# Squared-relu feed-forward: pairs of feature blocks by seven quadrant products

## The chip, the cores and the metric

One core of a Trainium2 chip runs the whole program. The metric is the time of one execution in microseconds (us), as the median of several runs. The core's engines each have an instruction queue that is worked off in order: PE (TensorE, matmuls), PEld (its weight loads), ACT (ScalarE), DVE (VectorE), POOL (GpSimd) and SP (which issues the DMAs). An instruction that waits for another engine holds up everything behind it in its own queue.

## What is computed

A network of two blocks on 512 tokens of width 1024, in fp32. The second block has two layers, and each ends in the feed-forward that the change concerns:

```
h = rms_norm_2(x, ffn_norm_g[layer])
x = x + jnp.square(jax.nn.relu(h @ w_ff1[layer])) @ w_ff2[layer]
```

`w_ff1` is 1024 x 4096 and `w_ff2` 4096 x 1024. The 4096 features are taken as 32 blocks of 128.

## The kernel before

**Products.** Each fp32 operand is kept as a high part (its cast to fp32r) and a low part (the rest), and each product is three matmuls, high by high, high by low, low by high (`mm3`, lines 163 to 165). A weight is loaded as fp32 into one of 3 buffers `raw` (`load`, DMA on SP), then `cut` makes the high part by a cast on ACT (line 150) and the low part by a subtraction on DVE (line 151), both 128x1024, in one of 5 buffers `ws`. `split_to` does the same for activations (cast at line 169, subtraction at line 170).

**The feed-forward** (`ffn2`, one call a layer, stages 6 and 9 of the program). The normalised tokens lie transposed in `hT`, as [128, 2 parts, 8 blocks of the width, 512 tokens]. The up-product of one feature block (`up`) is 8 x 3 matmuls of a 128x128 weight by 512 tokens. Its relu runs on ACT (line 1487, out of a PSUM bank), the square on DVE (line 1488), the split on ACT and DVE. `ff_head` has done tokens 256 to 511 of blocks 0 to 2 ahead; `ffn2` first does their tokens 0 to 255 ("the heads", 3 x 24 matmuls of 256 columns), then block 3, and from there on block 4, down-product of blocks 0 to 3, blocks 5 to 7, block 8, down-product of blocks 4 to 7, and so on. A down-product (`down`) of four blocks is 2 halves of the width x 4 blocks x 4 token tiles x 3 = 96 matmuls of 512 columns, and at the end of each half DVE adds four banks to x (line 1511). In layer 0 a generator `fill` runs the next layer's memory keys between the ups of the later blocks. The last down-product goes token by token (`down_last`).

**Order.** The order on each engine is fixed when the program is built, by a scheduler with its own estimates; the program's text is only its input. PSUM has six `acc` banks and two `tr` banks. `nrm` holds scratch tiles, two buffers to a tag; the tags `xn` and `gb` also hold the r tiles of the heads.

Of the kernel before, what the change touches and what calls it, by code (L numbers as in the profile page):

```python
# [94 lines left out]
class Net:  # L95
# [1380 lines left out]
    def ffn2(self, l, fill=None):  # L1476
        a, nc = self.a, self.nc
        W1, W2 = a["w_ff1_2"][l], a["w_ff2_2"][l]
        NF, CH = 32, 4
        with self.tc.tile_pool(name=f"ff2_{l}", bufs=8) as acts, \  # L1480
                self.tc.tile_pool(name=f"ff2t_{l}", bufs=3) as tmp, self.tc.tile_pool(name=f"ff2w_{l}", bufs=2) as ws2:
            A = {}

            def up_evac(f, b, r=None):
                n = S if r is None else 256
                r = tmp.tile([P, S], F32, tag="r", name=self.nm("r")) if r is None else r
                nc.scalar.activation(r[:, :n], b[:, :n], AF.Relu)
# [20 lines left out]
            def down(c, first, last):  # L1508
# [4 lines left out]
                if last:  # L1513
                    self.down_last(W2, ks, A, tail, None, ws2)
                else:
                    self.down(W2, ks, A, tail)

            ups([0, 1, 2], True)
            ups([3])
            for c in range(NF // CH):  # L1520
# [157 lines left out]
```

## Time and profile before

| | |
|---|---|
| median of 3 runs | 2920.12 us (2919.58 to 2923.12) |
| profiled execution | 2920.28 us |
| its span, first to last instruction | 2918.5 us |
| PE busy | 2857.1 us, 98% |
| DVE, ACT, POOL busy | 57%, 43%, 6% |
| mean granted TensorE clock | 0.997 |

The profiled execution lies 0.16 us above the median, and 1.8 us of it lie outside the span. Busy shares are means over the whole program.

### The profile page before, as it was taken

What the parts mean: (1) busy time and instruction counts of PE and PEld (TensorE: products, weight loads), DVE (VectorE), ACT (ScalarE), POOL (GpSimd) and SP (SyncE); (2) the same over time, 40 slices, a digit from 0 to 9 for tenths busy, and PEclk for the clock granted to TensorE, in tenths of its full rate; (3) what the DMA queues carried; (4) which work ended last, traced back from release to release, by engine and by line L of the source; (5) the groups of instructions that cost most, each with busy time, mean ns of one, the idle gap of its engine ahead of it and who ended that gap; (6) DMA issues with size and microseconds to landing.
All of it is one profiled execution on the core that took longest, in us unless ns stands there. A gap on an engine that the chain in (4) does not pass through costs nothing.

```text
span 2918.5 us, 36953 instructions
## 1 busy us (share of the span) xinstructions
PE 2857.1 (98%) x14150; PEld 2396.5 (82%) x14150; DVE 1675.1 (57%) x3186; ACT 1241.4 (43%) x2397; POOL 170.9 (6%) x257
## 2 busy tenths in 40 slices
PE   8999999999999999999999999999999999999999
PEld 6898888888888778878887878888888877888887
DVE  4334344646556886555567587745545578754443
ACT  3333333543334664433345476524233467532221
POOL 0000000000000321000002030000001022000000
PEclk9999999999999999999999999999999999999999
DMA  5332232333332243334243331234333342123332
GB/s 176 111 91 81 84 91 95 108 101 94 100 96 87 76 127 90 94 112 134 87 130 113 98 117 44 77 97 123 104 101 110 104 127 79 30 86 95 96 99 73
DMA packets 337845, 287.35 MB, mean 98 GB/s; under 512 B 13914, under 2 KB 275429, under 8 KB 337669
## 3 DMA queue, kind: packets, MB, share of 16 engines
q1 hardware_dynamic: 337668, 284.99, 32.3%
q8 instruction: 112, 1.84, 0.3%
q14 instruction: 65, 0.52, 0.1%
HBM read 272.34 MB, written 12.62 MB: 98 GB/s over the span
## 4 chain that ended last, share of the span: by engine, by line
PE 53%; DVE 7%; ACT 2%; DMA 2%; issue 1%; POOL 1%; SPq 0%; POOLq 0%; ACTq 0%; DVEq 0%
PE acc L163 16%; PE acc L165 16%; PE acc L164 16%; PE acc L1085 1%; PE acc L1098 1%; DMA raw<-in_ffn_w_up_dram 1%; PE tr L214 1%; PE tr L940 1%; DVE w L151 1%; PE acc L1230 1%; DMA raw<-in_w_in_dram 1%; PE acc L1424 1%; PE acc L1404 0%; DVE z L1142 0%; ACT w L150 0%
## 5 line engine op out<-in xcount | busy, mean ns | idle before, releaser
L151 DVE TENSOR_TENSOR w<-raw,w 128x1024 fp32r<-128x1024 f32 (+1 forms) x456 | 553.5, 1216 | 385.0 <-ACT w L150 383.7
L165 PE MATMUL acc<-hT,w 128*128 128x512 f32 (+1 forms) x1992 | 749.2, 376 | 3.7 <-DVE w L151 3.5
L163 PE MATMUL acc<-hT,w 128*128 128x512 f32 (+1 forms) x1992 | 752.3, 378 | 0.3 <-ACT hT L169 0.2
L164 PE MATMUL acc<-hT,w 128*128 128x512 f32 (+1 forms) x1992 | 750.1, 377 | 0.5 <-DVE hT L170 0.5
L150 ACT CAST w<-raw 128x1024 fp32r<-128x1024 f32 (+2 forms) x464 | 478.5, 1034 | 488.0 <-PE acc L165 397.5
L165 PEld LDWEIGHTS acc<-hT,w 128*128 128x128 f32 x1992 | 375.6, 189 | 72.6 <-DVE w L151 4.9
L164 PEld LDWEIGHTS acc<-hT,w 128*128 128x128 f32 x1992 | 375.8, 189 | 67.8 <-DVE hT L170 1.2
L163 PEld LDWEIGHTS acc<-hT,w 128*128 128x128 f32 x1992 | 375.2, 189 | 68.5 <-issue 0.7
L163 PE MATMUL acc<-w,act 128*128 128x512 f32 x896 | 349.7, 391 | 2.6 <-ACT act L169 1.5
L164 PE MATMUL acc<-w,act 128*128 128x512 f32 x896 | 349.1, 390 | 0.0
L165 PE MATMUL acc<-w,act 128*128 128x512 f32 x896 | 348.7, 390 | 0.0
L163 PE MATMUL acc<-w,hT 128*128 128x512 f32 (+2 forms) x768 | 286.5, 373 | 6.8 <-ACT hT L169 6.8
L165 PE MATMUL acc<-w,hT 128*128 128x512 f32 (+2 forms) x768 | 275.9, 359 | 0.6 <-DVE hT L170 0.6
L164 PE MATMUL acc<-w,hT 128*128 128x512 f32 (+2 forms) x768 | 275.2, 358 | 1.3 <-DVE w L151 1.3
L598 DVE SCALAR_TENSOR_TENSOR u<-acc,cw,u 128x511 f32<-128x511 f32 x192 | 143.6, 749 | 188.5 <-ACT u L596 185.3
L163 PEld LDWEIGHTS acc<-w,act 128*128 128x128 f32 x896 | 168.2, 188 | 39.5 <-ACT act L169 3.0
L165 PEld LDWEIGHTS acc<-w,act 128*128 128x128 f32 x896 | 168.1, 188 | 35.5 <-DVE act L170 0.6
L164 PEld LDWEIGHTS acc<-w,act 128*128 128x128 f32 x896 | 168.2, 188 | 34.7
L163 PEld LDWEIGHTS acc<-w,hT 128*128 128x128 f32 x768 | 162.3, 211 | 27.2 <-ACT hT L169 7.4
L164 PEld LDWEIGHTS acc<-w,hT 128*128 128x128 f32 x768 | 162.5, 212 | 18.0 <-issue 2.4
L165 PEld LDWEIGHTS acc<-w,hT 128*128 128x128 f32 x768 | 162.3, 211 | 15.7 <-DVE hT L170 0.9
L596 ACT ACTIVATE u<-acc,cw 128x512 f32<-128x512 f32 x96 | 74.9, 780 | 204.0 <-PE acc L165 204.0
(382 smaller groups left out, 3269.1 us busy)
## 6 DMA issues: line engine op xcount, KB each, us to landing
raw<-in_w_ff_dram SPq DMA_DIRECT2D x128, 512.0 KB
raw<-in_ffn_w_up_dram SPq DMA_DIRECT2D x96, 512.0 KB
raw<-in_attn_w_qkv_dram SPq DMA_DIRECT2D x72, 512.0 KB
raw<-in_ffn_w_down_dram SPq DMA_DIRECT2D x48, 512.0 KB
raw<-in_w_in_dram SPq DMA_DIRECT2D x40, 512.0 KB
raw<-in_lru_w_in_dram SPq DMA_DIRECT2D x16, 512.0 KB
raw<-in_w_out_dram SPq DMA_DIRECT2D x16, 512.0 KB
x<-in_x_dram SPq DMA_DIRECT2D x8, 512.0 KB
```

What stands on the lines that cost most here:

```text
L150: nc.scalar.copy(w[:, 0], raw)
L151: (lo or nc.vector).tensor_sub(w[:, 1], raw, w[:, 0].bitcast(F32))
L163: mm(out, sh, mh, start=first, stop=False)
L164: mm(out, sh, ml, start=False, stop=False)
L165: mm(out, sl, mh, start=False, stop=last)
L214: nc.tensor.transpose(b[:, j * P:(j + 1) * P], src[:, k * P:(k + 1) * P], self.ident)
L596: nc.scalar.activation(u, b, AF.Identity, bias=cw[:, 3, j:j + 1], scale=cw[:, 2, j:j + 1])
L598: nc.vector.scalar_tensor_tensor(u[:, s:], b[:, :S - s], cw[:, i, j:j + 1], u[:, s:], op0=ALU.mult, op1=ALU.add)
L940: nc.tensor.transpose(b[:, j * P:(j + 1) * P], src[:, j * P:(j + 1) * P], self.ident)
L1085: nc.tensor.matmul(o[:, oc:oc + dv], pT[:, k * P:(k + 1) * P], v(k), start=(k == 0), stop=(k == i))
L1098: nc.tensor.matmul(b[:, :w], QZ[:, h, m, i * P:(i + 1) * P], kT[:, h, :w], start=True, stop=True)
L1230: nc.tensor.matmul(b[:, :w], MT[:96, i, 0, h], MT[:96, :i + 1, 1, h], start=True, stop=True)
```

## The change

Blocks 4 to 31 are taken as 14 pairs a layer (28 in all). A pair of feature blocks by 1024 widths is a 2 x 2 of quadrants a11, a12 (the first block's lower and upper half of the width), a21, a22; the tokens are a 2 x 2 too: `B(w, i, j)` is half i of the width and tokens 256j on. Where the kernel before has eight products of quadrants, the pair now takes seven, with sums of quadrants as operands (the Winograd form of Strassen's scheme). One product is 4 x 3 matmuls of 128 weights by 256 tokens.

The sums of tokens are made once a layer (`combos`): four tiles R0 to R3 in buffers of `acts`, three of which end split as T0, T1, T2 (the tile `hc`), while `B(., 0, 1)` of hT is overwritten by R2. The sums of weights (s1 to s4) are made for every pair on POOL and split as `S12` and `S34`; of the two raw weights, all of the first (`w1`) and the upper half of the second (`w22`, a tile with one buffer) are split too. The products X, Z, Y, Wb, U lie in halves of two acc banks and in one tr bank; ACT copies two of them (c) and r1's first half out of PSUM, DVE adds up the rest, and relu and square become one `scalar_tensor_tensor` on DVE. Blocks 0 to 3 are done as before. `down_last` keeps the weights of its second half in buffers of `acts`.

```diff
     def ffn2(self, l, fill=None):
-        with self.tc.tile_pool(name=f"ff2_{l}", bufs=8) as acts, \
-                self.tc.tile_pool(name=f"ff2t_{l}", bufs=3) as tmp, self.tc.tile_pool(name=f"ff2w_{l}", bufs=2) as ws2:
+        v, gp, sc = nc.vector, nc.gpsimd, nc.scalar
+        hT = self.hT
+        with self.tc.tile_pool(name=f"ff2_{l}", bufs=8) as acts, self.tc.tile_pool(name=f"ff2h_{l}", bufs=1) as one, \
+                self.tc.tile_pool(name=f"ff2t_{l}", bufs=3) as tmp:
             A = {}
-
-            def up_evac(f, b, r=None):
-                n = S if r is None else 256
-                r = tmp.tile([P, S], F32, tag="r", name=self.nm("r")) if r is None else r
-                nc.scalar.activation(r[:, :n], b[:, :n], AF.Relu)
-                nc.vector.tensor_mul(r, r, r)
-                A[f] = acts.tile([P, 2, S], F32R, tag="act", name=self.nm("act"))
+            act = lambda name: acts.tile([P, 2, S], F32R, tag="act", name=self.nm(name))
+            tbuf = one.tile([P, 3 * 2048 + P], F32R, name=self.nm("hc"))[:, SHIFT:SHIFT + 3 * 2048]
+            T = tbuf.rearrange("p (n w k c) -> p n w k c", n=3, w=2, k=4)
+            R = [acts.tile([P, 4, 256], F32, tag="act", name=self.nm("hf")) for _ in range(4)]
+            def B(w, i, j):
+                return hT[:, w, 4 * i:4 * i + 4, 256 * j:256 * j + 256]
...
+            def combos():
+                for n, e in ((0, v), (1, v), (3, gp), (2, v)):
+                    e.tensor_add(R[n], B(0, n // 2, n % 2).bitcast(F32), B(1, n // 2, n % 2).bitcast(F32))
+                    if n == 1:
+                        v.tensor_sub(R[0], R[1], R[0])
+                        yield
+                gp.tensor_sub(R[1], R[3], R[1])
+                v.tensor_sub(R[3], R[3], R[0])
+                self.split_to(T[:, 0], R[0])
+                yield
+                v.tensor_sub(R[2], R[3], R[2])
+                self.split_to(T[:, 1], R[3])
+                yield
+                self.split_to(T[:, 2], R[1])
+                yield
+                sc.copy(B(0, 0, 1), R[2])
+                v.tensor_sub(B(1, 0, 1), R[2], B(0, 0, 1).bitcast(F32))
...
+            def out_act(f, r):
+                v.scalar_tensor_tensor(r, r, 0.0, r, op0=ALU.max, op1=ALU.mult)
+                A[f] = act("act")
                 self.split_to(A[f], r)
...
-            def ups(fs, split=False):
-                if split:
-                    for f in fs:
-                        w, r = self.head[f]
-                        b = self.bank()
-                        self.up(b, w, (0, 256))
-                        up_evac(f, b, r)
-                else:
-                    for f in fs:
-                        w = self.w_in(W1, f * P)
-                        b = self.bank()
-                        self.up(b, w)
-                        up_evac(f, b)
-                        if fill is not None and f > 6:
-                            next(fill, None)
-
...
+            def up_pair(f):
+                raw = [self.load(W1[:, g * P:g * P + P].rearrange("(k p) c -> p k c", p=P), (KD, P)) for g in (f, f + 1)]
+                w1 = self.cut(raw[0], (KD, P))
+                (a11, a12), (a21, a22) = ((r[:, :4], r[:, 4:]) for r in raw)
+                w22 = one.tile([P, 1024 + 16], F32R, tag="w22", name=self.nm("w22"))[:, 16:].rearrange("p (w k c) -> p w k c", w=2, k=4)
+                self.split_to(w22, a22)
+                S12, S34 = (self.ws.tile([P, 2, 2, 4, P], F32R, tag="w", name=self.nm("ws")) for _ in range(2))
+                f12, f34 = (self.nrm.tile([P, D], F32, tag=tag, name=self.nm("sf")).rearrange("p (n k c) -> p n k c", n=2, k=4)
+                            for tag in ("xn", "gb"))
+                s1, s2, s3, s4 = f12[:, 0], f12[:, 1], f34[:, 0], f34[:, 1]
+                gp.tensor_add(s1, a21, a22)
+                gp.tensor_sub(s2, s1, a11)
+                gp.tensor_sub(s4, a12, s2)
+                gp.tensor_sub(s3, a11, a21)
+                self.split_to(S12, f12)
+                self.split_to(S34, f34)
+                bx, bw = self.bank(), self.bank()
+                bu = self.tbank()
+                X, Z, Y, Wb, U = bx[:, :256], bx[:, 256:], bw[:, :256], bw[:, 256:], bu[:, :256]
+                def prod(out, st, mv, first=False, last=True):
+                    for k in range(4):
+                        for n, (x, y) in enumerate(((0, 0), (0, 1), (1, 0))):
+                            nc.tensor.matmul(out, st[:, x, k], mv(y)[:, k], start=first and k == n == 0,
+                                             stop=last and k == 3 and n == 2, skip_group_check=True)
+                t = lambda n: lambda w: T[:, n, w]
+                h = lambda i, j: lambda w: B(w, i, j)
+                c = tmp.tile([P, 2, 256], F32, tag="c", name=self.nm("c"), bufs=2)
+                u = tmp.tile([P, 2, 256], F32, tag="u", name=self.nm("u"), bufs=2)
+                r1, r2 = (tmp.tile([P, S], F32, tag="r", name=self.nm("r")) for _ in range(2))
+                prod(X, w1[:, :, :4], h(0, 0), True, False)
+                sc.copy(c[:, 0], X)
+                prod(Y, w22, h(0, 1), True, False)
+                prod(Z, S12[:, :, 0], t(0), False, False)
+                sc.copy(c[:, 1], Z)
+                prod(X, w1[:, :, 4:], h(1, 0), False, False)
+                sc.copy(r1[:, :256], X)
+                prod(Wb, S34[:, :, 0], t(2))
+                prod(U, S12[:, :, 1], t(1), True)
+                v.tensor_add(u[:, 0], U, c[:, 0])
+                v.tensor_add(u[:, 1], Wb, u[:, 0])
+                v.tensor_sub(r2[:, :256], u[:, 1], Y)
+                v.tensor_add(r2[:, 256:], u[:, 1], c[:, 1])
+                out_act(f + 1, r2)
+                prod(Z, S34[:, :, 1], h(1, 1))
+                v.tensor_add(r1[:, 256:], Z, u[:, 0])
+                out_act(f, r1)
+                if fill is not None and f > 6:
+                    next(fill, None)
+                    next(fill, None)
+            def rows_in_acts(k, c0):
+                raw = self.load(W2[k * P:(k + 2) * P, c0:c0 + 512].rearrange("(k p) c -> p k c", p=P), (2, 512))
+                out = []
+                for i in range(2):
+                    out.append(act("wl"))
+                    self.split_to(out[i], raw[:, i])
+                return out
...
-                    self.down_last(W2, ks, A, tail, None, ws2)
+                    self.down_last(W2, ks, A, tail, None, rows=rows_in_acts)
...
-            ups([0, 1, 2], True)
-            ups([3])
+            G = combos()
+            for f in range(3):
+                up_head(f)
+                next(G)
+            up_one(3)
+            for _ in G:
+                pass
             for c in range(NF // CH):
                 if c + 1 < NF // CH:
-                    ups([(c + 1) * CH])
-                down(c, c == 0, c == NF // CH - 1)
+                    up_pair((c + 1) * CH)
+                down(c, c == NF // CH - 1)
                 if c + 1 < NF // CH:
-                    ups(range((c + 1) * CH + 1, (c + 2) * CH))
+                    up_pair((c + 1) * CH + 2)
...
+    def down_last(self, W, ks, A, tail, post=None, pool=None, rows=None):
+        ws = []
+        for h in range(2):
+            ws.append([])
+            for k in ks[::2]:
+                if h and rows is not None:
+                    ws[h].extend(rows(k, h * 512))
+                else:
+                    w = self.w_rows(W, k, 2, h * 512, pool=pool if h else None)
+                    ws[h].extend(w[:, :, i] for i in range(2))
```

Three places where the order changes. On POOL, at the start of the second layer's feed-forward, there was nothing behind the last `ss` row of the norm. Now this stands there (sf are the weight sums of a pair, hf_21824 is R3, hf_21822 R1):

```order
L1550 TENSOR_TENSOR sf_21980<-raw_21967,raw_21969 128x512
L1547 TENSOR_TENSOR sf_21979<-raw_21969 128x512
L1548 TENSOR_TENSOR sf_21979<-sf_21979,raw_21967 128x512
L1549 TENSOR_TENSOR sf_21980<-raw_21967,sf_21979 128x512
L1500 TENSOR_TENSOR hf_21824<-hT 128x1024
L1504 TENSOR_TENSOR hf_21822<-hf_21824,hf_21822 128x1024
L1547 TENSOR_TENSOR sf_22240<-raw_22230 128x512
L1550 TENSOR_TENSOR sf_22241<-raw_22228,raw_22230 128x512
L1548 TENSOR_TENSOR sf_22240<-sf_22240,raw_22228 128x512
L1549 TENSOR_TENSOR sf_22241<-raw_22228,sf_22240 128x512
```

The fourth to sixth rows matter: pair 4's sums s1, s2, s4 stand ahead of the R3 add and of R1 = R3 - R1, and the sums of the next pair (raw_22228, raw_22230) follow.

DVE at the same place, before, from the last split of hT on (line 1488 is the square of a head, w are the down-product's weights):

```order
L170 TENSOR_TENSOR hT<-tr_20947,hT 128x4x128
L1488 TENSOR_TENSOR r_20871<-r_20871 128x512
L151 TENSOR_TENSOR w_21163<-raw_21161,w_21163 128x1024
L170 TENSOR_TENSOR act_21022<-r_20871,act_21022 128x512
L1488 TENSOR_TENSOR r_20914<-r_20914 128x512
L151 TENSOR_TENSOR w_21192<-raw_21190,w_21192 128x1024
L170 TENSOR_TENSOR act_21052<-r_20914,act_21052 128x512
L1488 TENSOR_TENSOR r_20955<-r_20955 128x512
```

DVE in the kernel after, from the second head's act on (hf_21821, hf_21823, hf_21824 are R0, R2, R3; hc is T; line 1517 is relu and square of heads 1, 2 and block 3 in turn; the last row rewrites hT):

```order
L172 TENSOR_TENSOR act_21885<-r_21739,act_21885 128x512
L1500 TENSOR_TENSOR hf_21823<-hT 128x1024
L1505 TENSOR_TENSOR hf_21824<-hf_21824,hf_21821 128x1024
L172 TENSOR_TENSOR hc_21820<-hf_21821,hc_21820 128x1024
L1517 SCALAR_TENSOR_TENSOR r_21780<-r_21780 128x512
L1508 TENSOR_TENSOR hf_21823<-hf_21824,hf_21823 128x1024
L172 TENSOR_TENSOR act_21921<-r_21780,act_21921 128x512
L172 TENSOR_TENSOR hc_21820<-hf_21824,hc_21820 128x1024
L1517 SCALAR_TENSOR_TENSOR r_21957<-r_21957 128x512
L172 TENSOR_TENSOR hc_21820<-hf_21822,hc_21820 128x1024
L172 TENSOR_TENSOR act_21960<-r_21957,act_21960 128x512
L1514 TENSOR_TENSOR hT<-hf_21823,hT 128x4x256
```

R3 - R0 (line 1505) overwrites R3 and so has to wait for POOL's R1 = R3 - R1; the nine rows behind it stand between it and the new hT.

PE at the same place, before: the last matmuls of block 4, then the down-product of blocks 0 to 3.

```order
L163 MATMUL acc_21126<-hT,w_21123 128x512
L164 MATMUL acc_21126<-hT,w_21123 128x512
L165 MATMUL acc_21126<-hT,w_21123 128x512
L163 MATMUL acc_21157<-w_21163,act_21022 128x512
L164 MATMUL acc_21157<-w_21163,act_21022 128x512
```

PE after, behind block 3 and behind pair 4's X product, which is left out (tr_21991 is U, acc_21990 holds Y and Wb, acc_21989 X and Z; the rows of act_21852 belong to the down-product):

```order
L1560 MATMUL tr_21991<-hc_21820,ws_21977 128x256
L1560 MATMUL acc_21990<-hT,w_3352_21974 128x256
L165 MATMUL acc_22096<-w_22102,act_21852 128x512
L165 MATMUL acc_22097<-w_22102,act_21852 128x512
L1560 MATMUL tr_21991<-hc_21820,ws_21977 128x256
L165 MATMUL acc_22098<-w_22102,act_21852 128x512
L165 MATMUL acc_22099<-w_22102,act_21852 128x512
L1560 MATMUL acc_21989<-hc_21820,ws_21977 128x256 x2
L1560 MATMUL acc_21990<-hT,w_3352_21974 128x256 x11
L1560 MATMUL acc_21989<-hc_21820,ws_21977 128x256 x10
L1560 MATMUL acc_21990<-hc_21820,ws_21978 128x256 x4
L1560 MATMUL acc_21989<-hT,w_21971 128x256 x12
```

The first Y matmul uses the new hT's high part, the row with x11 its low part; seven matmuls stand between X and that row. The last two rows show the order in every pair: Wb has four matmuls between the last of Z and the second part of X, which waits for ACT's copy of Z.

## Rows read from the trace of the kernel before

**Rows 1.** The page, part 1: busy us of each engine, share, instructions.

```profile
PE 2857.1 (98%) x14150; PEld 2396.5 (82%) x14150; DVE 1675.1 (57%) x3186; ACT 1241.4 (43%) x2397; POOL 170.9 (6%) x257
```

**Rows 2.** Windows inside the second up-and-down stage: busy us and instructions per engine.

```profile
2640.00:2683.50 43.50, 43.50 (x194) 36.02 (x193) 20.41 (x25) 12.44 (x16) 0.00 (x0) 1.00 0.32 97
2573.70:2597.00 23.30, 23.30 (x139) 20.78 (x138) 12.60 (x15) 10.02 (x16) 0.00 (x0) 1.00 0.31 91
```

**Rows 3.** Matmuls by shape: count, then busy us and mean ns of one.

```profile
L163 PE MATMUL acc<-hT,w 128*128 128x512 f32 x1720 | 676.2, 393 | 0.1
...
L163 PE MATMUL acc<-hT,w 128*128 128x256 f32 x272 | 76.4, 285 | 0.2 <-ACT hT L169 0.2
```

**Rows 4.** TensorE in order of time, start of the second stage: start, duration.

```profile
2573.72 0.28 PE L163 MATMUL acc<-hT,w 128*128 128x256 f32 x1
...
2582.36 0.40 PE L163 MATMUL acc<-hT,w 128*128 128x512 f32 x1
...
2585.11 0.39 PE L163 MATMUL acc<-hT,w 128*128 128x512 f32 x1
...
2588.51 0.39 PE L163 MATMUL acc<-hT,w 128*128 128x512 f32 x1
```

**Rows 5.** VectorE groups by shape.

```profile
L151 DVE TENSOR_TENSOR w<-raw,w 128x1024 fp32r<-128x1024 f32 x448 | 546.5, 1222 | 353.7 <-ACT w L150 352.5
...
L170 DVE TENSOR_TENSOR act<-r,act 128x512 fp32r<-128x512 f32 x64 | 43.8, 684 | 2.1 <-ACT act L169 2.1
...
L231 DVE SCALAR_TENSOR_TENSOR xn<-x,ss,gb 128x512 f32<-128x512 f32 x32 | 22.9, 748 | 10.6 <-POOL ss L204 9.9 <-DMA tz<-fz 0.8
...
L170 DVE TENSOR_TENSOR xh<-xc,xh 128x512 fp32r<-128x512 f32 x8 | 7.2, 904 | 2.4 <-ACT xh L169 2.4
...
L960 DVE TENSOR_TENSOR on<-acc,rs 128x256 f32<-128x256 f32 x16 | 6.7, 417 | 0.3
```

**Rows 6.** ScalarE groups by shape.

```profile
L150 ACT CAST w<-raw 128x1024 fp32r<-128x1024 f32 x448 | 467.6, 1046 | 484.8 <-PE acc L165 396.0 <-issue 34.5 <-DMA raw<-in_attn_w_qkv_dram 18.7
...
L169 ACT CAST act<-r 128x512 fp32r<-128x512 f32 x64 | 39.6, 618 | 2.3 <-DVE r L1488 2.3
...
L942 ACT COPY pT<-tr 128x256 f32<-128x256 f32 x24 | 8.4, 366 | 1.6 <-PE tr L940 1.3
```

**Rows 7.** GpSimd groups by shape.

```profile
L782 POOL TENSOR_TENSOR r<-r,y 128x512 f32<-128x512 f32 x8 | 12.6, 1581 | 5.9 <-DVE y L778 4.3 <-PE acc L165 1.4
...
L151 POOL TENSOR_TENSOR w<-raw,w 128x512 fp32r<-128x512 f32 x8 | 12.2, 1526 | 25.5 <-ACT w L150 15.9 <-PE acc L165 9.5
...
L1205 POOL TENSOR_TENSOR x<-x,gqk 128x768 f32<-128x768 f32 x6 | 11.0, 1836 | 16.7 <-DVE x L1200 16.7
```

**Rows 8.** ScalarE in order of time: relu of head 0, tokens 0 to 255.

```profile
2576.80 0.38 ACT L1487 ACTIVATE r<-acc 128x256 f32<-128x256 f32 x1 [2.50 <-PE acc L165]
```

**Rows 9.** VectorE in order of time: what follows that relu.

```profile
2577.22 0.69 DVE L1488 TENSOR_TENSOR r<-r 128x512 f32<-128x512 f32 x1 [4.98 <-ACT r L1487]
```

**Rows 10.** A wait of TensorE for a ScalarE cast, all engines in order of time.

```profile
931.11 0.62 ACT L169 CAST act<-u 128x512 fp32r<-128x512 f32 x1 [2.40 <-DVE u L606]
...
931.55 0.73 PE L163 MATMUL acc<-w,act 128*128 128x512 f32 x2
...
931.78 0.19 PEld L163 LDWEIGHTS acc<-w,act 128*128 128x128 f32 x1 [0.26 <-ACT act L169]
...
932.12 0.40 PE L164 MATMUL acc<-w,act 128*128 128x512 f32 x1
```

**Rows 11.** TensorE after two long waits, in order of time.

```profile
34.50 0.58 PE L163 MATMUL acc<-w,hT 128*128 128x256 f32 x1 [5.27 <-ACT hT L169]
...
1017.63 0.80 PE L165 MATMUL acc<-xh,w 128*128 128x512 f32 x1 [3.90 <-POOL w L151]
```

**Rows 12.** Windows behind those waits: busy us, granted clock, DMA.

```profile
34.40:39.80 5.40, 4.72 (x16) 4.13 (x17) 3.87 (x4) 3.14 (x5) 0.00 (x0) 0.50 0.69 207
...
1017.60:1022.60 5.00, 4.97 (x12) 3.91 (x13) 5.00 (x6) 4.33 (x6) 1.42 (x1) 0.50 0.33 97
```

More of the change, by code (lines that the diff above doesn't have):

```diff
@@ L25 @@
 EPS = 1e-6
+SHIFT = 112
 TINY = 368
@@ L1479, in ffn2 @@
         NF, CH = 32, 4
-        with self.tc.tile_pool(name=f"ff2_{l}", bufs=8) as acts, \
-                self.tc.tile_pool(name=f"ff2t_{l}", bufs=3) as tmp, self.tc.tile_pool(name=f"ff2w_{l}", bufs=2) as ws2:
+        v, gp, sc = nc.vector, nc.gpsimd, nc.scalar
+        hT = self.hT
+        with self.tc.tile_pool(name=f"ff2_{l}", bufs=8) as acts, self.tc.tile_pool(name=f"ff2h_{l}", bufs=1) as one, \
+                self.tc.tile_pool(name=f"ff2t_{l}", bufs=3) as tmp:
             A = {}
-            def up_evac(f, b, r=None):
-                n = S if r is None else 256
-                r = tmp.tile([P, S], F32, tag="r", name=self.nm("r")) if r is None else r
-                nc.scalar.activation(r[:, :n], b[:, :n], AF.Relu)
-                nc.vector.tensor_mul(r, r, r)
-                A[f] = acts.tile([P, 2, S], F32R, tag="act", name=self.nm("act"))
-                self.split_to(A[f], r)
-            def ups(fs, split=False):
-                if split:
-                    for f in fs:
-                        w, r = self.head[f]
-                        b = self.bank()
-                        self.up(b, w, (0, 256))
-                        up_evac(f, b, r)
-                else:
-                    for f in fs:
-                        w = self.w_in(W1, f * P)
-                        b = self.bank()
-                        self.up(b, w)
-                        up_evac(f, b)
-                        if fill is not None and f > 6:
-                            next(fill, None)
-            def down(c, first, last):
@@ new lines, in out_act, with up_head, up_one @@
+            def out_act(f, r):
+                v.scalar_tensor_tensor(r, r, 0.0, r, op0=ALU.max, op1=ALU.mult)
+                A[f] = act("act")
+                self.split_to(A[f], r)
+            def up_head(f):
+                w, r = self.head[f]
+                b = self.bank()
+                self.up(b, w, (0, 256))
+                sc.activation(r[:, :256], b[:, :256], AF.Relu)
+                out_act(f, r)
+            def up_one(f):
+                w = self.w_in(W1, f * P)
+                b = self.bank()
+                self.up(b, w)
+                r = tmp.tile([P, S], F32, tag="r", name=self.nm("r"))
+                sc.activation(r, b, AF.Relu)
+                out_act(f, r)
@@ L1509, in tail, with down @@
+            def rows_in_acts(k, c0):
[5 more added lines that the diff above has]
+                return out
+            def down(c, last):
                 def tail(t, h, b):
@@ L1542, in down @@
         weave((self.down_gen(W, ks, A, tail), 1))
-    def down_last(self, W, ks, A, tail, post=None, pool=None):
-        ws = [[self.w_rows(W, k, 2, h * 512, pool=pool if h else None) for k in ks[::2]] for h in range(2)]
+    def down_last(self, W, ks, A, tail, post=None, pool=None, rows=None):
[8 more added lines that the diff above has]
+                    ws[h].extend(w[:, :, i] for i in range(2))
         end = self.next_g is None and post is None
@@ L1554, in tok @@
                 for i, k in enumerate(ks):
-                    w = ws[h][i // 2]
+                    w = ws[h][i]
                     self.mm3(b, A[k][:, 0, t * P:(t + 1) * P], A[k][:, 1, t * P:(t + 1) * P],
-                             w[:, 0, i % 2], w[:, 1, i % 2], i == 0, i == len(ks) - 1)
+                             w[:, 0], w[:, 1], i == 0, i == len(ks) - 1)
             yield
```

## The prediction

> **What bounds the kernel now.** I read the page first: PE is busy 98% of the span [rows 1], so time can only come from fewer or shorter matmuls, and any wait that is put on PE costs its full length. Then the windows inside the second layer's feed-forward: in 43.5 us, one down-product with its four ups, PE is busy 43.5, DVE 20.4, ACT 12.4 and POOL nothing, at clock 1.00; the start of the stage (2573.7 to 2597) is as full on PE, with DVE at 12.6 of 23.3 [rows 2]. There is no wait on PE to remove here. Then the matmuls by shape [rows 3]: their durations (393 and 285 ns) overlap and say nothing of pace, so I take the pace from the starts in order of time [rows 4]. The 72 matmuls of 256 columns from 2573.72 to 2582.36 take 8.64 us, 120 ns each; the 15 of 512 columns from 2585.11 to 2588.51 take 226.7 ns each. Half the columns cost 53% of the time.
>
> **The products.** A pair takes 2 x 8 x 3 = 48 matmuls of 512 before, 10.88 us, and 7 x 4 x 3 = 84 of 256 after, 10.08 us. That is 0.80 us a pair and **-22.4 us** for 28 pairs. [rows 3] has 272 such matmuls for each of the three lines, so the shape itself is not new. The Trainium skill ("TensorE: Matmul & The Clock Gate", section "Back-to-back issue gap") gives N / 2.4 + 2.5 ns for an isolated gap at full clock, 109.2 and 215.8 ns. By it, as an estimate, a pair would gain 1.19 us, all pairs 33.3, and the sum below would end 11 us lower; the trace is 11 ns above it at both widths, so the measured paces decide.
>
> **Waits in each pair.** After a wait PE loses more than the wait: the cast that began at 931.11 ended at 931.73, the load for the matmul due at 931.78 began then, and the next started at 932.12 instead of 932.01 (two paces after 931.55) [rows 10]. So I count 0.16 us from a release to the matmul that it frees. (a) X's second part waits for ACT's copy of Z. From Z's last start: 0.28 to its end [rows 3], 0.04 to ACT (head 0's relu starts 0.04 after the last matmul's end, 2573.72 + 23 x 0.12 + 0.28 = 2576.76, at 2576.80 [rows 4, 8]), copy 0.37 [rows 6], 0.16: 0.85. PE covers it with Wb's four matmuls and comes due after 0.60. Lost 0.25 us, 28 times: +7.0. (b) In the second pair of two that follow each other, Z waits for ACT's copy of X, which stands behind the first pair's act cast, and that behind DVE's sums and its relu-and-square, themselves one low-part split late. Worked out with 0.42 a PSUM sum, 0.75 a square [rows 5] and 0.62 a cast [rows 6], it comes 0.2 late, 12 times: +2.4. Together **+9.4 us**, with 0 (the copies are quicker or the wait is hidden) and 16 as bounds.
>
> The other new work lies beside PE. On DVE a pair now takes low parts of 3 x 1.22 + 0.68, five sums of 0.42, two squares of 0.75 and two acts of 0.68, 9.3 us, against 5.2 before (2 x 1.22, and four of 0.68 to 0.69); a group of two pairs and a down-product thus goes from 20.4 us [rows 2] to some 29 of its 42. ACT gets about 1.6 us more a pair, POOL four sums of 1.53 to 1.58 [rows 7]. That cover is gone if DVE or POOL run much slower together (rival 3).
>
> **The start of the stage, twice.** Call 2573.72 zero [rows 4]; layer 0 has the same order on the engines. PE works from stock until X of pair 4 ends: heads 8.64, block 3 5.44, X 1.44, so 15.5. Y then needs the rewritten hT.
> - POOL: s1 lies in the buffer of head 0's r and waits until head 0's act is split. The relu is at 3.08 to 3.46 [rows 8], DVE starts at 3.50 [rows 9]; square 0.75, the R0 add 1.22, act 0.68 [rows 5]: 6.2. Behind s1 stand s2, s4 (1.55 each [rows 7]), the R3 add and R1 = R3 - R1. No row has POOL with 1024 columns: twice the 512 row is 3.1, the pace of the 768-column row gives 2.45 [rows 7]. I take 3.1, since the operands are plain as in the 512 rows. Five operations make 10.9 us, and R1 is done at 17.1.
> - DVE: R3 - R0 must wait for that, and nine instructions follow up to hT's low part. Six of 1024 columns, two squares and two acts: 6 x 1.22 + 2 x 0.75 + 2 x 0.68 = 10.2 [rows 5]. hT is ready at **27.3**.
> - PE: resumes at 27.5 with 67 matmuls of 256 columns, 8.0 us, so pair 4 ends at 35.5; without the wait at 15.5 + 72 x 0.12 = 24.2. Four matmuls of the down-product were slipped in, worth 0.9. Lost: 10.4 us.
> - Clock: PE stood idle 5.27 us before 34.50 and 3.90 us before 1017.63 [rows 11], and the granted clock was 0.50 in the 5.4 and 5.0 us around and after these restarts [rows 12]: 2.5 us lost. The wait here is longer, so I add 2.5.
>
> That is 12.9 a layer, **+25.8 us**. Bounds: 8.1 a layer with POOL at the lower pace (8.6 us instead of 10.9) and no slower clock; 16.3 if DVE beside POOL takes 904 ns instead of 684 [rows 5], which makes its 10.2 us 13.5 and adds a little to the restart.
>
> The Trainium skill ("GPSIMD Engine Reference", section 3.1) measures 4497 ns for an add of 2048 fp32 columns on GpSimd against 2293 on VectorE. As an estimate 1024 columns would be 2.25 us and 512 1.12; POOL's five would take 7.9 and the sum would come out 6 us lower. The trace's 1.53 to 1.58 for 512 columns [rows 7] is above that, and decides.
>
> **Layer 0's fill.** Scratch of the norms and the pairs' weight sums share buffers, so in the new order s1 of pair 22 waits for transposes that stand directly ahead of its X. s1, s2, cast and low part take 2 x 1.55 + 1.05 + 1.22 [rows 5 to 7], 5.4 us, against 26 matmuls that PE has, 3.1: 2.5 lost. Pair 12 has a like wait (about 2), and a key weight's low part stands behind a pair's sums on DVE (about 1.5). Together **+6 us**, bounds 0 and 10.
>
> **The end, twice.** The last down-product needs pair 30's acts at once and then four low parts of second-half weights, all behind the pair's sums on DVE: sums end 0.9 after the pair, two squares 2.4, two acts 3.8, four parts 6.5, against 22 matmuls (5.0): 1.5 lost, **+3 us** for both, bounds 0 and 4.
>
> Sum: -22.4 + 9.4 + 25.8 + 6 + 3 = +21.8 on the profiled execution's 2920.3, which stands 0.2 above the median: **2942 us**. All lower ends give 2914, all upper ends 2961 (16, 32.6, 10, 4).
>
> **The rivals.**
> 1. The token sums come in time, and the change gains. For it: DVE has room at the stage's start (12.6 of 23.3 us busy [rows 2]), and if POOL's queue were short only DVE's own ten instructions would count. Against it: even with POOL ending at 6.2 + 5 the chain would reach 21, past 15.5; it decides when hT is ready by 15.5. Then the start costs nothing and the time is 2942 - 25.8 = 2916, or 2907 without the waits in each pair.
> 2. About even: the start costs its lower bound (16), the waits in pairs 4, fill and end 3: 2921. For it: every one of these terms has its cheaper price in a row. Against it: all have to be cheap together.
> 3. DVE or POOL fall behind in every group. For it: 904 ns instead of 684 beside POOL [rows 5], and S12's low part of the second pair stands ahead of the x sums of the down-product, with about 1.4 us to spare. Against it: POOL works 12 of 42 us only. With 1 to 2 us on each of 14 groups: 2956 to 2970.
> 4. PE's pace with 256 columns could be worse where the weight loads crowd it: PEld is busy 36 of 43.5 us already [rows 2]. But the heads are at 120 ns with a load for each matmul [rows 4], so I give it no term.
>
> **How the numbers follow.** My sum 0.62 (2927 to 2955 by itself), rival 1 0.16, rival 2 0.10, rival 3 0.12. The time given is that of the likeliest, 2942. For 8 in 10 the range reaches from 2911, inside rival 1, to 2960. A measurement of this kernel can tell about 0.2%, 5.8 us. Slower by more: my sum and rival 3, 0.74; within: rival 2, 0.10; faster by more: rival 1 mostly, 0.16.
>
> **What would show it.** Right: in the trace after, two gaps of PE of about 10 us in all, each about 15 us behind the heads, ended by DVE's rewritten hT, with POOL working from 6 to 17 us after the first head and granted clock 0.5 behind; starts 120 ns apart in the products; small gaps ahead of X's second part that ACT ends. Wrong: no such gap (then rival 1), x sums or S12 splits as releasers of PE in every group (rival 3), or another pace than 120 ns.

## The result, and the profile after

The changed kernel takes 2960.68 us (2959.32 to 2961.13) against 2921.62 us before: ratio 1.0133, 95% interval 1.0115 to 1.015, slower by 39 us. Slower was forecast, by 21.8 us; the range ended at 2960. The profiled execution's span is 2958.8 us, 40.3 above before's. Its page, part 1, as in [rows 1]:

```profile
PE 2856.3 (97%) x15158; PEld 2431.9 (82%) x15158; DVE 1859.3 (63%) x3406; ACT 1298.7 (44%) x2493; POOL 367.6 (12%) x373
```

PE has less work than before, is busy as long (2856.3 us for 2857.1 [rows 1]) and ends 40 us later, so waits and clock have to be looked for. I cut both executions at the same events: the first head's relu (it starts the stage) and the first of the sums that each down-product half adds to x (DVE's work, so the cut says when DVE came to it, not only when PE was through). The first head's relu of the second layer, ScalarE in order of time, as in [rows 8]:

```profile
2611.34 0.38 ACT L1526 ACTIVATE r<-acc 128x256 f32<-128x256 f32 x1 [2.50 <-PE acc L167]
```

From here to the end of the span it is 347.5 us, and from 2576.80 [rows 8] it was 341.7: the second layer loses 5.8. The first layer's relu stands at 1885.37 now and 1885.92 before. So 35 us are lost between the two relus, and 2 of these lie in the attention stages behind the first feed-forward. In pieces, in us:

| stretch | before | after | difference | forecast |
|---|---|---|---|---|
| layer 0, relu to first x sum | 26.8 | 44.6 | +17.8 | +17.5 |
| layer 0, the five groups that follow | 230.0 | 253.4 | **+23.4** | **+1.5** |
| layer 0, rest | 88.4 | 80.1 | -8.3 | |
| layer 1, relu to first x sum | 25.5 | 46.1 | +20.6 | +17.5 |
| layer 1, six groups | 261.1 | 253.6 | -7.5 | -5.4 |
| layer 1, rest | 55.1 | 47.8 | -7.3 | |

(The forecast of a start is its 12.9 plus 4.6, because a pair of 10.08 us now stands ahead of the first down-product instead of one block of 5.44; that of a group is two pairs with their waits, -0.9, and the fill's 6 for the five. The 4.6 come back in the rows "rest", where one pair now stands for three blocks.)

**The start.** TensorE in order of time in the second layer, only rows with a wait (in brackets: idle before, and what ended it):

```profile
2629.52 0.58 PE L1560 MATMUL tr<-hc,ws 128*128 128x256 f32 x1 [5.56 <-ACT hc L171]
...
2631.76 0.58 PE L1560 MATMUL acc<-hT,w 128*128 128x256 f32 x1 [1.66 <-ACT hT L1513]
...
2635.89 2.72 PE L1560 MATMUL acc<-hT,w 128*128 128x256 f32 x11 [1.20 <-DVE hT L1514]
```

The last two are the new hT. Zero of the forecast is 2611.34 - 3.08 = 2608.26. GpSimd in order of time:

```profile
2614.26 2.21 POOL L1547 TENSOR_TENSOR sf<-raw 128x512 f32<-128x512 f32 x1 [10.82 <-DVE act L172]
2616.55 1.62 POOL L1548 TENSOR_TENSOR sf<-sf,raw 128x512 f32<-128x512 f32 x1
2618.25 2.15 POOL L1549 TENSOR_TENSOR sf<-raw,sf 128x512 f32<-128x512 f32 x1
2620.36 2.85 POOL L1500 TENSOR_TENSOR hf<-hT 128x1024 f32<-128x1024 f32 x1
2623.29 3.20 POOL L1504 TENSOR_TENSOR hf<-hf,hf 128x1024 f32<-128x1024 f32 x1
```

s1 starts at 6.0 (forecast 6.2) and R1 is done at 18.2 (17.1). VectorE in order of time, of the rows that were listed with the change:

```profile
2615.24 1.78 DVE L1517 SCALAR_TENSOR_TENSOR r<-r 128x512 f32<-128x512 f32 x1
...
2616.95 2.30 DVE L1502 TENSOR_TENSOR hf<-hf,hf 128x1024 f32<-128x1024 f32 x1
...
2620.87 3.43 DVE L1500 TENSOR_TENSOR hf<-hT 128x1024 f32<-128x1024 f32 x1
...
2626.53 1.23 DVE L1505 TENSOR_TENSOR hf<-hf,hf 128x1024 f32<-128x1024 f32 x1 [2.23 <-POOL hf L1504]
...
2634.62 1.22 DVE L1514 TENSOR_TENSOR hT<-hf,hT 128x1024 fp32r<-128x1024 f32 x1
```

The fourth row waits for POOL and starts at 18.3, the last ends at 27.6 (forecast 27.3). The first three rows show something else: a square took 1.78, and two sums of 1024 columns 2.30 and 3.43 us while POOL worked, for 0.75 and 1.22 in [rows 5]. They did no harm here, since POOL was later. Windows (busy us and instructions by engine, granted clock, DMA) behind the wait, and one group further on:

```profile
2624.00:2629.00 5.00, 0.00 (x0) 0.00 (x0) 2.77 (x4) 2.47 (x3) 2.50 (x1) 1.00 0.00 0
2629.00:2634.00 5.00, 2.82 (x7) 2.21 (x8) 5.00 (x6) 4.46 (x7) 0.00 (x0) 0.50 0.00 0
2634.00:2639.50 5.50, 4.30 (x21) 3.94 (x20) 5.50 (x7) 0.00 (x0) 0.00 (x0) 0.52 0.01 3
2657.40:2699.70 42.30, 41.56 (x262) 37.47 (x263) 31.86 (x40) 15.67 (x23) 12.96 (x8) 1.00 0.32 101
```

The clock is at 0.50 to 0.52, the lower of its two levels, for 10 us, not for the 5 that I took from [rows 12]. Up to 2635.89 PE had only nine matmuls to do. In layer 0 PE has the same three waits (5.56, 1.66 and 1.21), and the clock is back by the time it can go on:

```profile
1903.00:1908.00 5.00, 2.79 (x7) 2.20 (x8) 5.00 (x6) 4.50 (x7) 0.00 (x0) 0.50 0.00 0
1908.00:1914.00 6.00, 4.79 (x35) 4.21 (x34) 6.00 (x7) 0.37 (x1) 0.00 (x0) 0.93 0.00 0
```

What it cost is read from the 67 matmuls of pair 4 behind the last of these waits, up to the down-product's next one, in order of time, in layer 1 and then in layer 0:

```profile
2645.58 0.40 PE L166 MATMUL acc<-w,act 128*128 128x512 f32 x1
```

```profile
1909.93 1.54 PE L1560 MATMUL acc<-hT,w 128*128 128x256 f32 x11 [1.21 <-DVE hT L1514]
...
1918.11 0.40 PE L166 MATMUL acc<-w,act 128*128 128x512 f32 x1
...
1930.72 0.50 PE L165 MATMUL acc<-w,act 128*128 128x512 f32 x1 [1.08 <-DVE x L1600]
...
1940.35 3.00 PE L1560 MATMUL acc<-hT,w 128*128 128x256 f32 x24
```

From 2635.89 it is 9.7 us and from 1909.93 8.2, where 67 x 0.12 are 8.0: the clock cost about 1.7 and 0.1 us, not 2.5 twice. PE then waits about 1 us for an x sum, which I had not counted (1.08 in layer 0, 1.02 in layer 1): DVE is late with it. So the two starts in the table hold lateness of DVE that cost PE little, and the rows "rest" are shorter by it. PE's own event is the first matmul behind this down-product, which is pair 6's X now (1940.35, and 2667.80 below) and was block 5's in both layers of the kernel before:

```profile
1924.14 0.39 PE L163 MATMUL acc<-hT,w 128*128 128x512 f32 x1
...
2615.03 0.39 PE L163 MATMUL acc<-hT,w 128*128 128x512 f32 x1
```

From the relu it was 38.2 us in either layer; now it is 55.0 in layer 0 and 56.5 in layer 1. Less the 4.6 of the pair that stands ahead, PE lost 12.1 and 13.6 us, 25.7 in all, for a forecast of 25.8.

**A group.** The row from 2657.40 to 2699.70 above: 42.3 us, nearly without a wait on PE, against 43.5 [rows 2]. TensorE in order of time, one pair and the start of the next (24 matmuls of X and Y, 16 of Z and Wb, the second part of X, and so on):

```profile
2667.80 3.01 PE L1560 MATMUL acc<-hT,w 128*128 128x256 f32 x24
...
2670.64 2.00 PE L1560 MATMUL acc<-hc,ws 128*128 128x256 f32 x16
...
2672.65 1.69 PE L1560 MATMUL acc<-hT,w 128*128 128x256 f32 x12
...
2674.17 1.09 PE L1560 MATMUL acc<-hc,ws 128*128 128x256 f32 x8
...
2675.10 1.52 PE L1560 MATMUL tr<-hc,ws 128*128 128x256 f32 x12
...
2676.46 1.58 PE L1560 MATMUL acc<-hT,ws 128*128 128x256 f32 x12
...
2677.88 3.02 PE L1560 MATMUL acc<-hT,w 128*128 128x256 f32 x24
```

The pair takes 10.08 us with its waits in it. X and Y go at 118 ns; the twelve of U, which take the sums T out of hc, at 113, and Wb's last eight at 116. The sixteen with Z take 2.01 us where 16 x 0.114 were 1.82, so 0.2 us are X's wait for ACT's copy, as worked out (0.25). The faster pace and the waits cancel. The next pair (from 2677.88) takes as long, so the wait forecast for the second of two pairs does not appear.

**The fill in layer 0.** In the five groups PE waits 18 us in all, in many pieces; the longest is that of pair 6's Z. TensorE, then ScalarE, in order of time:

```profile
1949.19 1.22 PE L1560 MATMUL acc<-hc,ws 128*128 128x256 f32 x4 [5.83 <-ACT c L1568]
```

```profile
1946.60 0.63 ACT L203 ACTIVATE sq<-mem 128x512 f32<-128x512 f32 x1 [8.93 <-DMA mem<-in_mem_dram]
...
1948.79 0.35 ACT L1568 COPY c<-acc 128x256 f32<-128x256 f32 x1
```

Z waits for ACT's copy of X. The copy stands behind the fill's square of the second memory tile (L203), and that waits 8.9 us for its DMA. SyncE's queue, in order of time:

```profile
1938.21 0.34 SPq L177 DMA_DIRECT2D gb<-in_mem_norm_g_dram  x1
1943.11 0.33 SPq L986 DMA_DIRECT2D mem<-in_mem_dram  x1
```

The gain row (gb) is issued at 1938.21, just when DVE has split S34 out of its scratch (tag gb), and the second tile (mem) at 1943.11, when DVE's norm of the first tile is through. So a fill that was free on PE before is now chained through the pairs' scratch, SP, ACT's order, and PE. Windows over the groups with the fill, after and then before:

```profile
1930.00:2140.00 210.00, 191.75 (x1128) 169.01 (x1128) 141.46 (x212) 74.98 (x113) 51.97 (x35) 0.96 0.32 102
```

```profile
1930.00:2140.00 210.00, 210.00 (x936) 173.39 (x936) 105.67 (x160) 66.52 (x93) 0.00 (x0) 1.00 0.34 101
```

PE is busy 192 of 210 us at a clock of 0.96. Before, it was 210 at 1.00. Cut in pieces of 5 us, the clock is below 0.9 in four places: from 1945 to 1955, behind the wait of 5.8, and near 1985, 2067 and 2117, behind waits of 1.8, 1.8 and two of 1.2.

### The profile page after: what moved, and what is told of

Same layout as the page of the kernel before. It is cut to its first block, busy times and chain, and to the rows that moved or that the text cites. A ratio compares the mean times of both kernels' runs of the same rounds, so it can differ in the third digit from the quotient of the medians.

```text
span 2958.8 us, 39474 instructions
## 1 busy us (share of the span) xinstructions
PE 2856.3 (97%) x15158; PEld 2431.9 (82%) x15158; DVE 1859.3 (63%) x3406; ACT 1298.7 (44%) x2493; POOL 367.6 (12%) x373
## 5 line engine op out<-in xcount | busy, mean ns | idle before, releaser
L153 DVE TENSOR_TENSOR w<-raw,w 128x1024 fp32r<-128x1024 f32 x424 | 530.4, 1253 | 346.2 <-ACT w L152 344.8
L152 ACT CAST w<-raw 128x1024 fp32r<-128x1024 f32 (+2 forms) x432 | 445.8, 1034 | 383.4 <-PE acc L167 257.0
L165 PE MATMUL acc<-hT,w 128*128 128x512 f32 (+1 forms) x1544 | 577.6, 375 | 0.2 <-ACT hT L171 0.2
L167 PE MATMUL acc<-hT,w 128*128 128x512 f32 (+1 forms) x1544 | 574.7, 372 | 3.0 <-DVE w L153 3.0
L166 PE MATMUL acc<-hT,w 128*128 128x512 f32 (+1 forms) x1544 | 575.7, 373 | 0.5 <-DVE hT L172 0.5
L165 PE MATMUL acc<-w,act 128*128 128x512 f32 x864 | 341.8, 397 | 11.8 <-DVE x L1600 6.5
L166 PE MATMUL acc<-w,act 128*128 128x512 f32 x864 | 338.2, 391 | 0.0
L167 PE MATMUL acc<-w,act 128*128 128x512 f32 x864 | 337.5, 391 | 0.0
L167 PEld LDWEIGHTS acc<-hT,w 128*128 128x128 f32 x1544 | 291.8, 189 | 54.0 <-DVE w L153 3.9
L165 PEld LDWEIGHTS acc<-hT,w 128*128 128x128 f32 x1544 | 291.4, 189 | 51.0 <-issue 0.7
L166 PEld LDWEIGHTS acc<-hT,w 128*128 128x128 f32 x1544 | 291.7, 189 | 49.9 <-DVE hT L172 1.2
L206 POOL TENSOR_TENSOR ss<-ss,small 128x1 f32<-128x1 f32 x60 | 45.2, 753 | 1519.5 <-DVE ss L205 1519.5
L165 PEld LDWEIGHTS acc<-w,act 128*128 128x128 f32 x864 | 163.5, 190 | 53.4 <-DVE x L1600 12.5
L167 PEld LDWEIGHTS acc<-w,act 128*128 128x128 f32 x864 | 163.0, 189 | 34.6 <-DVE act L172 0.4
L166 PEld LDWEIGHTS acc<-w,act 128*128 128x128 f32 x864 | 163.1, 189 | 32.4
```

The lines of the kernel that those rows point to most:

```text
L152: nc.scalar.copy(w[:, 0], raw)
L153: (lo or nc.vector).tensor_sub(w[:, 1], raw, w[:, 0].bitcast(F32))
L165: mm(out, sh, mh, start=first, stop=False)
L166: mm(out, sh, ml, start=False, stop=False)
L167: mm(out, sl, mh, start=False, stop=last)
L206: nc.gpsimd.tensor_tensor(ss[:, 3:4], ss[:, 2:3], self.mhalf[:, :1], op=ALU.pow)
```

## The experiments

The scheduler orders every one of these kernels anew, so a difference of a few us belongs to the edit and the order that came of it together.

**Which layer, and is it the fill?** Three kernels. `layer1_only` keeps the old `ffn2` for layer 0:

```diff
-                net.ffn2(l, fill if s == 6 else None)
+                (net.ffn2 if l else net.ffn2_old)(l, fill if s == 6 else None)
```

> The first layer's feed-forward is as before the change, the second's as after. Theory A (what the change loses is mostly a collision with the memory-key fill, which only the first layer's feed-forward carries): 2927 us, about 6 us above the kernel before, since the stretch from the first head's relu to the end is 347.5 us in the profile after and 341.7 before. Rival B (pairs lose the same in both layers, and the first layer only shows it more): 2940 us, half of the 39.

2926.45 us, ratio 1.0021 (1.0011 to 1.003): 5 us, as the pieces say. `before_late` and `after_late` take the fill out of the feed-forward of either kernel:

```diff
-                net.ffn2(l, fill if s == 6 else None)
+                net.ffn2(l, None)
```

> The kernel before with the memory keys of the second layer not woven into the first layer's feed-forward but done in one piece behind it. It is the yardstick for the next kernel: both theories expect some 5 to 15 us more than before (its products take the same time wherever they stand, its chain of norms and transposes then stands open), so 2927 to 2936 us.

> The changed kernel with the memory keys done in one piece behind the first layer's feed-forward. Theory A: each layer then loses what the second layer lost, about 6 us, so 12 us above the kernel before with the same move. Rival B: still 30 to 39 us above it.

2934.67 and 2945.43 us: the change costs 10.8 us without the fill in the pairs, and 39 with it. Theory A holds: some 28 us of the loss go with the fill. The groups without the fill, window in `after_late`:

```profile
1930.00:2140.00 210.00, 208.73 (x1311) 186.34 (x1310) 155.42 (x190) 80.17 (x110) 65.64 (x40) 1.00 0.33 101
```

PE is busy 208.7 of 210 us at full clock, with more instructions than in the window above.

**The start.** `pairs_from_6` and `singles_4_5` give the token sums more time. The edit of the second:

```diff
+            next(G)
+            up_one(4)
+            up_one(5)
             for _ in G:
                 pass
 ...
-                if c + 1 < NF // CH:
+                if 0 < c < NF // CH - 1:
                     up_pair((c + 1) * CH)
```

> The changed kernel with blocks 4 and 5 taken singly, as before, and pairs from block 6 on, so that the token sums have the first down-product's 22 us to come ready. If the wait at the start is as predicted (15.9 us a layer as measured from the first relu to the first x sum, with its slower clock), it goes away: about 30 us less than the changed kernel, less 1 us a layer for the pair given up, 2931 us. Rival: the sums still hold up DVE, and the wait moves to the first down-product's x sums or to pair 6; then 2945 us or more.

2946.86 us. This form had the single blocks behind the whole of `combos`, so that they read hT after its quarter had been overwritten: their products are not the reference's, and they wait for the same hT as pair 4 did. `singles_4_5` mends that, so its time alone is used.

> The changed kernel with blocks 4 and 5 taken singly ahead of the first down-product, and hT's quarter overwritten only behind them; pairs from block 6 on. Theory (the start's loss is the token sums' chain): the sums then have 10.9 us of two single blocks and 21.8 us of down-product to come ready, PE does not wait, and a layer gets back 15.9 us less 1 for the pair given up: 2961 - 30 = 2931 us. Rival (DVE is too full there whatever stands on PE): the wait moves to the down-product's x sums, and less than half comes back, 2946 us or more.

2943.64 us, 17 of the 30 us. In layer 1 the stage got 9.4 us shorter (338.1 from the relu to the end), and PE's waits of 5.56, 1.66 and 1.20 became one of 2.02 (for a weight's low part on DVE), at clock 1.00. In layer 0 the stretch up to the first x sum got 7.9 us shorter; what follows it, with the fill still in the pairs, kept its length (332.3 for 333.5 us). The 30 expected were read off x sums, DVE's lateness included.

`sums_on_dve` takes POOL's two token sums to DVE (`gp` to `v` in `combos`):

> The changed kernel with the two token sums of POOL (the R3 add and R1 = R3 - R1) on DVE. If POOL's queue is what makes hT late (R1 done 18.2 us after the first head began, hT 27.6): DVE has 20 instructions to do without a wait, some 19 us, hT is ready at about 23, 4 to 5 us a layer come back, 2952 us. Rival: DVE's own work sets it, with the two sums added; 2960 us or more.

2957.32 us, less than expected back. hT was ready at 25.3 instead of the 23 expected: the weight sums that stayed on POOL still slowed DVE, R0's subtraction to 2.30 us, a square to 1.78.

**What of the fill?** `hold_ws` and `hold_banks` are `after_late` with only the buffers held:

```diff
+        t = [self.ws.tile([P, 2, KD, P], F32R, tag="w", name=self.nm("hold")) for _ in range(2)]
+        cols = [w[:, 0, 0, :1].bitcast(F32) for w in t]
 ...
+            cols = [self.bank()[:, :1] for _ in range(2)]
```

> The changed kernel with the memory keys done late (2945 us), and two of the five weight buffers merely held in the first layer's feed-forward over the 13 steps in which the fill holds them for its transposed memory; no work of the fill with it. Theory A1 (the pairs, which take three weight buffers each, starve when the fill holds two): most of the 18 us by which the woven fill is dearer than this comes back on top, 2957 us or more. A2 (the two PSUM banks that the fill holds) and A3 (what the fill's instructions stand in front of on ACT, DVE and the DMA queue): 2945 to 2948 us.

> As hold_ws, but two of the six acc banks are held for the steps in which the fill sums its keys and values. A2: 2957 us or more, with PE waiting for the x sums on DVE ahead of pairs and down-products. A1 and A3: 2945 to 2948 us.

2949.32 and 2946.7 us. From layer 0's first x sum to its last four it is 291.5 us in `after_late`, 291.7 and 291.4 here: neither A1 nor A2. `hold_ws` stands 1 us above its expected range, for a reason that stays open. `fill_norms_early` goes at A3: `singles_4_5` with four steps `next(fill, None)` between blocks 3, 4, 5 and the first down-product.

> singles_4_5 (2944 us) with the fill's first four steps, its loads, norms and transposes, moved ahead of the first pair, into blocks 3 to 5; its products and the rest stay in the pairs. Theory A3 (what is dear is that the norm part stands in front of the pairs' instructions on ACT and the DMA queue and takes their scratch buffers): the 3.8 us wait for ACT's copy, the two waits around the transposes and the slower clock behind them go, 2933 us. Rival A4 (the keys' products and the x sums that wait behind them): less than 4 us come back, 2940 us or more.

2926.76 us, 17 back, more than expected: the same stretch of layer 0 goes from 332.3 to 318.3 us. What is left there is some 8 us of PE's waits between 1990 and 2080, around the keys' products.

**POOL or DVE.** `no_pool` has the four weight sums on DVE as well as the token sums:

> The changed kernel with all its sums on DVE and none on POOL. While POOL sums, DVE's subtractions take 1.1 to 2.3 us for 0.7 to 1.2, so by the profile POOL's help is nearly paid back. Theory (DVE has room in the groups, 29.5 of 40 us with that slowing): no new waits in the second layer's groups, hT at the start ready at about 25 us instead of 27.6, 2950 to 2958 us. Rival (DVE fills up): each group waits for it, 2975 us or more.

2935.19 us: 25 less, which neither expected. VectorE by shape in the second layer's groups, 2660 to 2900, in the changed kernel, and then in `no_pool` (L1549 is one of the four sums):

```profile
L153 DVE TENSOR_TENSOR w<-raw,w 128x1024 fp32r<-128x1024 f32 x34 | 51.9, 1526 | 29.7 <-ACT w L152 29.7
...
L1600 DVE TENSOR_TENSOR x<-x,acc 128x512 f32<-128x512 f32 x44 | 28.7, 682 | 1.3 <-PE acc L167 1.3
...
L172 DVE TENSOR_TENSOR act<-r,act 128x512 fp32r<-128x512 f32 x22 | 22.9, 1082 | 0.0
...
L172 DVE TENSOR_TENSOR w<-raw,w 128x512 fp32r<-128x512 f32 x11 | 13.0, 1183 | 6.9 <-ACT w L171 6.9
```

```profile
L153 DVE TENSOR_TENSOR w<-raw,w 128x1024 fp32r<-128x1024 f32 x36 | 44.0, 1223 | 24.6 <-ACT w L152 24.6
...
L1600 DVE TENSOR_TENSOR x<-x,acc 128x512 f32<-128x512 f32 x48 | 31.8, 686 | 7.9 <-PE acc L167 7.9
...
L172 DVE TENSOR_TENSOR act<-r,act 128x512 fp32r<-128x512 f32 x22 | 14.2, 686 | 0.0
...
L1549 DVE TENSOR_TENSOR sf<-raw,sf 128x512 f32<-128x512 f32 x11 | 7.6, 692 | 0.4
...
L172 DVE TENSOR_TENSOR w<-raw,w 128x512 fp32r<-128x512 f32 x11 | 7.6, 691 | 6.0 <-ACT w L171 6.0
```

Without POOL, DVE takes 1.22 instead of 1.53 for a weight's low part, 0.69 instead of 1.08 for an act's, 0.69 instead of 1.18 for w22's. The x sums, which read PSUM, are the same (0.68). A group of `no_pool`:

```profile
2676.70:2718.60 41.90, 41.88 (x265) 37.73 (x264) 31.66 (x47) 16.01 (x23) 0.00 (x0) 1.00 0.33 101
```

DVE is busy 31.7 us in a group of 41.9, with eight more sums in it; in the changed kernel it was 31.9 of 42.3. POOL spared DVE nothing. hT is ready at 22.0 us of the stage instead of 27.6, since no queue of POOL stands ahead of R3 - R0, and layer 0's stretch behind the first x sum falls from 333.5 to 320.6. Of the 25 us, 5 lie at layer 0's start, 13 in this stretch and 7 in layer 1.

**A version that gains.** `layer1_singles` and `late_pairs` take pairs where no fill is: in layer 1 from 6, and in layer 0 not at all, or from block 20.

> The first layer's feed-forward as before the change, the second's with blocks 4 and 5 single and pairs from 6. From the profiles: the second layer cost 5.8 us more than before in the changed kernel, and blocks 4 and 5 single took 9.7 us off it, so 4 us less than the kernel before: 2917 us. Rival (those 4 us are the difference of two executions and not of the kernels): 2921 us or more.

> As layer1_singles, but the first layer takes pairs too, from block 20 on, where the fill is done; token sums at the stage's start, R2 kept until block 19 is done. If a pair without the fill is worth the 0.62 us that the second layer's groups show (42.26 instead of 43.5 us): six pairs -3.7, against 1 to 3 us for the sums at the start, 1 for the wait behind the rewritten quarter and 1.4 at the end: 2916 to 2919 us. Rival (the start of the first layer is dearer than that): 2921 us or more.

2918.07 (ratio 0.9989, 0.998 to 0.9997) and 2917.98 us (0.9991, 0.9982 to 1.0): as expected, the first just clear of no change and the second at the edge. In `late_pairs`, R2 lies in w22's buffer until it is needed. The last three put the sums on DVE. The edit of `pairs_12_no_pool` against `late_pairs`, in which s2 to s4 and the token sums move likewise and the fill is drawn forward into blocks 3 to 11:

```diff
-            first = 6 if l else 20
+            first = 6 if l else 12
 ...
-                gp.tensor_add(s1, a21, a22)
+                v.tensor_add(s1, a21, a22)
```

> late_pairs (2918 us) with all sums on DVE. If POOL's sums slow DVE by as much as they spare it (DVE is as busy with and without them, 29.6 against 29.8 of 40 us in the second layer's groups), groups take 41.9 instead of 42.3 us and the starts lose less of their two 1.1 us waits: 2913 to 2915 us. Rival (the groups' 0.3 us were chance): 2918 us.

> fill_norms_early (2927 us) with all sums on DVE. Theory C (in the first layer, too, the slowing of DVE and POOL by each other is what makes the fill's remaining products and x sums late, 10 us of waits between 1997 and 2076): 2913 to 2917 us, half of those waits gone. Rival (what is left is the order in which the fill's instructions stand, whoever sums): 2922 us or more.

> late_no_pool with the fill drawn together into blocks 3 to 11, so that the first layer takes pairs from block 12 on, ten instead of six. By 0.78 us a pair without POOL (41.94 instead of 43.5 us a group): 3 us less than late_no_pool, 2910 to 2912 us, below the kernel before by 0.3%. Rival: two steps of the fill to a single block put new waits there, and 3 us or more are lost again, 2914 us or more.

`late_no_pool` 2911.77 us (ratio 0.9969, 0.9956 to 0.9981), below what was expected. `norms_early_no_pool` 2921.44 us, 5.3 less than with POOL, nearly at the rival's 2922: the stretch of layer 0 falls from 318.3 to 312.7 us, but waits for the fill's products stay. `pairs_12_no_pool` 2910.05 us, ratio 0.9962 (0.995 to 0.9975): faster than before by 11 us, though only 1.7 below `late_no_pool`, within what the medians can tell. The same window of its layer 0, single blocks first and then pairs, and PE's waits from 1870 to 2240 (us in total, times, longest):

```profile
1930.00:2140.00 210.00, 209.87 (x1207) 183.84 (x1206) 150.35 (x242) 84.39 (x119) 0.00 (x0) 1.00 0.35 107
```

```profile
PE acc L165 <- ACT act L171: 1.4, 1, 1.4
PE tr L216 <- DVE xn L233: 1.2, 2, 0.7
PE acc L166 <- DVE w L153: 0.5, 1, 0.5
```

## Why the prediction was right in kind and short by half

- **What bounds it.** Right: PE was full, and every wait that came cost its length.
- **The products, -22.4, and the waits in each pair, +9.4.** Right within 5 us: a group takes 42.3 us for 43.5, 0.62 gained a pair where -22.4 + 9.4 means 0.46. Of the two waits, X's for ACT's copy was there and the second pair's was not; the pace was better than the heads' 120 ns on the operands that come from T. The pairs alone gain more (10.08 us for 10.88); 42.3 less two of them leaves 22.1 for the down-product, which took 21.8 before. The Trainium skill ("TensorE: Matmul & The Clock Gate", section "Back-to-back issue gap") gives 109 ns for an isolated gap; no product shown here went so fast (113).
- **The start, +25.8.** The mechanism and its times were right to about a microsecond (6.0, 18.2 and 27.6 for 6.2, 17.1 and 27.3): POOL took 12.2 us for its five sums instead of 10.9, and DVE 9.3 behind it instead of 10.2. PE lost 25.7 us. That it comes so close is in part luck: the clock cost 1.8 us instead of 5, and two waits for x sums, 2.1 us, were not in the sum. The stretches in the table show 3 us more, because DVE is late with the x sum that ends them.
- **Layer 0's fill, +6, bounds 0 and 10.** This is the step that failed. The five groups with the fill lost 23.4 us against a forecast of 1.5, and without the fill in the pairs (`after_late`) PE hardly waits in them; by the medians the fill in the pairs costs 28 us. I priced three waits on PE for scratch and low parts, with the shared scratch at pairs 12 and 22 only. I left out that the fill's loads and norms stand in the same queues of SP and ACT as the pairs' copies, that at pair 6 a load of the fill waits for the pair's scratch (PE's wait of 5.8 us), that such waits bring a slower clock with them (0.96 over the 210 us, at most 8 us, less where PE waits meanwhile), and that DVE ran slower than its rows of before. The runs give some 14 us to the order of the norms (`fill_norms_early`). They put 6 (`norms_early_no_pool`) to 13 (`no_pool`) on POOL's sums; these overlap. How the rest divides between the keys' products and the x sums behind them was not tried.
- **The end, +3.** PE's wait for the act there is 1.4 us in layer 0 and 1.3 in layer 1, as worked out.
- **Rival 3** (DVE and POOL behind in every group) was right in its cause and wrong in its effect: DVE did slow down, but had room in the second layer's groups. It was the start's queue and the fill where the slowing reached PE. Rival 1 could not come in time, as argued: even without POOL's queue (`no_pool`) hT was ready at 22.0, past 15.5. Of rival 2's cheap prices those of the clock and of the second pair's wait appeared, the others did not. Rival 4 fell: the pace was no worse.

## What to carry to other kernels

Fewer products help a kernel with a full PE only if the sums around them have a place: count, for every stage that shares a queue or a scratch tag with the new work, what its instructions will stand behind, not only what each costs. A helper engine has spared nothing until the other engine's time is measured beside it: here the same sums on DVE alone left DVE as busy in the second layer's groups and the kernel 25 us shorter. Where a new operand needs a long chain once, do enough of the old work first to cover it.

## What the hardware showed unexpectedly

- With POOL summing part of the time, DVE's low parts of weights, of w22 and of acts, both operands in SBUF, took 1.25 to 1.7 times as long in the mean, and one sum 2.8 times (3.43 for 1.22 us); its sums out of PSUM kept their 0.68 us. POOL's s4 took 2.04 us in the mean in the second layer, s3 1.51. The Trainium skill ("GPSIMD Engine Reference", section 1) says that GpSimd's SBUF interfaces are shared with VectorE and contend with its instructions that have two SBUF inputs; this trace agrees, and the one row of before that showed it (904 instead of 684 ns, [rows 5]) hid its full size: it is a mean of eight, and one of these took 1.78 us.
- The same 256-column product takes 113 to 116 ns with its tokens from T and 118 to 120 from hT. T begins 112 elements into its buffer; whether the address is the cause was not tried.
- Behind the same three waits (5.56, 1.66 and 1.2 us) the clock stayed at its lower level (0.50) for 10 us in layer 1 and for about 6 in layer 0, where single waits of 5.3 and 3.9 us had kept it there for some 5 [rows 11, 12]. Why the two layers differ was not tried. In the groups with the fill it also fell behind waits of 1.8 us.
